# A two-layer attention and retention trunk: first rotation read from PSUM, a block's projections in column parts, and sines and weight squares issued at other steps

## The chip, the core and the metric

The kernel runs on one core of one Trainium2 chip. A core has five engines that each work through their own instructions in order and wait for each other by semaphores: PE (matrix products, with a separate row for its weight loads, PEld), DVE (vector work), ACT (scalar functions with lookup tables), POOL, and SP, which here only issues DMA transfers. The metric is device time in microseconds (us); lower is better.

## The reference

Two layers over 2048 tokens of width 1024, then a last norm. Each layer computes

```python
hn = rms_norm(x, norm_gain)
aq, ak, av, ag, rq, rk, rv, rg = split(hn @ w_in)      # eight sections of 512 columns
ya = chunked_rel_attention(aq, ak, av, rel_bias)       # 8 heads x 64, chunks of 64 tokens, own chunk + 8 before
yr = chunkwise_retention(rq, rk, rv, cos, sin)         # 4 heads x 128, rotary phases, decay, group norm
y = concat([ya * silu(ag), yr * silu(rg)])
x = x + y @ w_out
```

The retention turns rq and rk by angles that grow with the position: `[t1*c - t2*s, t1*s + t2*c]` on the two halves of a head's 128 columns. Everything is float32 in and out, so the kernel forms each float32 product from three half-precision products: high by high, low by high and high by low.

The weights are not used as they stand: the kernel scales each block of weights by the root of its mean square before it is cut into a high and a low half. So each weight section has to be squared and summed before it can be converted.

## The kernel before

**Tiling.** A layer l is worked in four column groups s, and a group holds one retention head and two attention heads. For each group the tokens are worked in four row blocks n of 512 tokens, each made of four token tiles of 128. A block (l, s, n) has two dense stages. `dense_T` (L608) makes four tiles with the columns on the partitions and 512 tokens along the row: j = 0 is q, 1 is k, 2 is rq, 3 is rk; each takes 24 matmuls (eight sections of the inner dimension, three half-precision products). `dense_V` (L738) makes four tiles, one for each token tile, that hold v, rv and the gates; 24 matmuls each (L752). The attention (`attention` L778: scores S at L800 and L801, output o at L820 to L822) and the retention (`retention` L884, its products r at L860) of the block before run between these matmuls. The first block (0, 0, 0) is special: `first` is set, and q and k are made in eight parts of 128 columns (L712), since the normalised and transposed token tiles hTh and hTl arrive one by one.

**Order.** All instructions are issued by one Python program, and each engine works in the order issued. A round is some eight matmuls. At the end of a round `tick()` (L598) calls the functions that `later(k, fn)` (L595) has put off by k rounds. Work for later blocks runs as generators that are pushed with a number of steps and pulled some steps a round: `prep_T`, `prep_V` and `prep_O` load, square, scale and split weights, `prep_Omax` (L494) does the squares of the output weights, `tables` (L83) makes the angles' cosines and sines for a row block and writes them to DRAM, and the norms of later token tiles. PE, DVE, ACT and POOL follow this order; the issues on SP follow it until the end of the first `dense_V` and are ordered by a planner afterwards.

**PSUM.** The dense tiles have two buffers (psD), the scores one (psS), small results four (psR); in the first block rq and rk also use psR. A dense_V tile is evacuated by ACT (L760 to L763) and then by three "rests" on DVE (L766, L768, L770), after which its buffer is free.

**The rotation.** For rq and rk (L656 to L703) ACT copies the tile out of PSUM to `raw` (L662). Two DMAs on SP swap its halves into `swp` (L666, L667). DVE multiplies raw by the cosine table tabc and swp by the sine table tabs and adds (three operations at L670), ACT makes the upper half-precision part (L673), DVE the lower (L676); rq gets a third part from ACT (L679), and rk is transposed by DMA into kt (L683). Tabc and tabs are read back from DRAM by two DMAs (L616, L617).

**Weight squares.** `sumsq` (L306) squares a section on ACT (L309) with a sum along the row; `lowp` (L314) casts the sum to bfloat16 on DVE (L316); `allsum` (L320) sums over partitions with a small matmul against ones (L323) and DVE reads the result (L325). The sections of the T weights (q, k, rq, rk) and of the V weights (v, rv, gates) are prepared this way. In `square` (T) the cast directly follows the square, and so it does in `prep_V`:

```python
self.sq[j] = lowp(sumsq(self.sts[j], nm, self.g.h[:, j]), nm)
```

For the output weights `prep_Omax` squares eight sections one after the other, and adds each sum to the one before on DVE (L504, L506).

## Time and profile before

| | us |
|---|---|
| median of 3 runs | 2094.44 (2092.88 to 2094.84) |
| the profiled execution | 2094.75 |
| its span | 2092.8, which leaves 1.95 outside it |
| PE busy | 2004.4 (96%) |
| DVE busy | 1343.8 (64%) |
| ACT busy | 1141.3 (55%) |
| POOL busy | 432.9 (21%) |

The chain of work that ended last is PE's for the most part, and the rest of it is waiting for DMA, DVE and ACT. How to read the rows in the prediction: in a timeline row stand the start, the duration, the engine, the line of the program, the operation, the result and what it is made from, its shape, and how many instructions the row holds; in brackets how long the engine had been idle before it and what released it. A row of the waits gives the total, the number and the longest. SPq is the queue on which SP issues DMAs. The matmul of 128x512 is followed by the next after 0.216 us although each lasts 0.38: they are pipelined.

### The profile page before, as it was taken

The numbers are of one execution on the slowest core, as the hardware profiler recorded it, in microseconds if no ns is written. First come the engines' busy times: TensorE is split into PE (matmuls) and PEld (weight loads), VectorE is DVE, ScalarE is ACT, GpSimd is POOL, SyncE is SP. The second block draws the span as 40 slices with busy tenths as digits, with TensorE's granted clock in tenths as the row PEclk, the third lists the DMA queues.
The fourth block names the chain that finished last, engine by engine and source line by source line (L and its number), as shares of the span: only waits on it lengthen the run. The fifth ranks groups of instructions, "written<-read, shape, count | busy, mean of one in ns | idle before, by whom it ended". The sixth has DMA issues, their size and how long they took to land.

```text
span 2092.8 us, 39599 instructions
## 1 busy us (share of the span) xinstructions
PE 2004.4 (96%) x14014; PEld 1049.4 (50%) x14014; DVE 1343.8 (64%) x4031; ACT 1141.3 (55%) x2522; POOL 432.9 (21%) x509
## 2 busy tenths in 40 slices
PE   6888999999999999998999999999999999998998
PEld 4344455555555555444444555555555555554443
DVE  7676666666656666576654666666666667656643
ACT  7455665556565654455444546554655565455432
POOL 1022222222122212121000222222222222222100
PEclk9999999999999999999999999999999999999999
DMA  8767674557476764599965556655655776558874
GB/s 247 171 127 162 136 166 114 115 112 159 110 169 133 161 166 99 113 211 260 219 185 113 120 102 142 130 121 106 155 123 118 178 156 162 117 100 183 212 199 123
DMA packets 645702, 313.65 MB, mean 150 GB/s; under 512 B 459232, under 2 KB 602080, under 8 KB 645504
## 3 DMA queue, kind: packets, MB, share of 16 engines
q1 hardware_dynamic: 645504, 311.12, 66.4%
q8 instruction: 110, 1.80, 0.4%
q14 instruction: 88, 0.72, 0.1%
HBM read 123.26 MB, written 41.98 MB: 79 GB/s over the span
## 4 chain that ended last, share of the span: by engine, by line
PE 55%; DMA 7%; DVE 5%; ACT 3%; issue 1%; SPq 1%; POOL 0%; POOLq 0%; DVEq 0%; ACTq 0%
PE dT L731 18%; PE dV L752 15%; PE dO L1105 12%; DMA pT<-pq 2%; PE r L860 2%; PE S L801 2%; PE S L800 2%; PE o L820 1%; PE o L821 1%; PE o L822 1%; DVE sc L804 1%; DMA swp<-rot 1%; DMA yhy<-rhy 1%; ACT sc L807 1%; ACT pq L809 1%
## 5 line engine op out<-in xcount | busy, mean ns | idle before, releaser
L810 POOL TENSOR_TENSOR pq<-sc,pq 128x640 f16<-128x640 f32 (+4 forms) x256 | 323.8, 1265 | 1175.9 <-issue 590.7
L807 ACT ACTIVATE sc<-sc,mq,cT 128x640 f32<-128x640 f32 (+4 forms) x256 | 218.5, 853 | 558.1 <-DVE mq L806 413.7
L752 PE MATMUL dV<-whV,hTh 128*128 128x512 f16 x1024 | 354.5, 382 | 13.0 <-DVE gt L770 12.8
L731 PE MATMUL dT<-hTh,whT 128*128 128x512 f16 x1008 | 349.4, 382 | 14.7 <-DMA hTh<-hTl 9.6
L752 PE MATMUL dV<-wlV,hTh 128*128 128x512 f16 x1024 | 354.1, 381 | 0.0
L752 PE MATMUL dV<-whV,hTl 128*128 128x512 f16 x1024 | 354.0, 381 | 0.0
L731 PE MATMUL dT<-hTl,whT 128*128 128x512 f16 x1008 | 346.6, 379 | 0.0
L731 PE MATMUL dT<-hTh,wlT 128*128 128x512 f16 x1008 | 346.6, 379 | 0.0
L752 PEld LDWEIGHTS <-hTh 128*128 128x128 f16 x2048 | 197.3, 98 | 227.7 <-DVE gt L770 16.4
L731 PEld LDWEIGHTS <-whT 128*128 128x128 f16 x2016 | 192.9, 98 | 221.6 <-issue 24.1
L804 DVE CUSTOM_DVE_ANT_0 sc<-S,bias 128x640 f32<-128x640 f32 (+4 forms) x256 | 188.4, 736 | 78.8 <-PE S L801 61.1
L1105 PE MATMUL dO<-whO,yly 128*128 128x512 f16 x512 | 194.1, 379 | 2.4 <-DMA yly<-rly 2.4
L1105 PE MATMUL dO<-whO,yhy 128*128 128x512 f16 x512 | 194.0, 379 | 1.2 <-DVE gt L770 0.6
L1105 PE MATMUL dO<-wlO,yhy 128*128 128x512 f16 x512 | 194.0, 379 | 0.0
L809 ACT ACTIVATE pq<-sc 128x640 f16<-128x640 f32 (+4 forms) x256 | 171.5, 670 | 10.9 <-DMA pT<-pq 3.0
L1105 PEld LDWEIGHTS <-yhy 128*128 128x128 f16 x1024 | 99.6, 98 | 115.1 <-issue 0.8
L752 PEld LDWEIGHTS <-hTl 128*128 128x128 f16 x1024 | 99.7, 98 | 105.0 <-issue 2.8
L800 PE MATMUL S<-k,q 128*128 128x128 f16 (+3 forms) x592 | 143.1, 268 | 7.9 <-DVE mq L804 7.9
L731 PEld LDWEIGHTS <-wlT 128*128 128x128 f16 x1008 | 97.2, 98 | 101.8 <-issue 1.1
L820 PE MATMUL o<-v,pT 128*128 128x65 f16 x1120 | 129.6, 193 | 10.2 <-DMA pT<-pq 9.7
L801 PE MATMUL S<-k,q 128*128 128x128 f16 (+3 forms) x592 | 130.5, 268 | 0.0
L820 PEld LDWEIGHTS <-pT 128*128 128x128 f16 x1120 | 105.3, 97 | 49.2 <-DMA pT<-pq 21.3
(350 smaller groups left out, 3352.7 us busy)
## 6 DMA issues: line engine op xcount, KB each, us to landing
q<-qq SPq DMA_DIRECT2D x128, 128.0 KB, 2.7
yyy<-y_d SPq DMA_DIRECT2D x32, 512.0 KB, 4.6
stT<-in_w_in_dram SPq DMA_DIRECT2D x27, 512.0 KB, 4.8
stV<-in_w_in_dram SPq DMA_DIRECT2D x26, 512.0 KB, 4.5
k<-kk SPq DMA_DIRECT2D x128, 64.0 KB, 2.0
swp<-rot SPq DMA_DIRECT2D x64, 128.0 KB, 2.5
tabc<-tab SPq DMA_DIRECT2D x32, 256.0 KB, 2.7
tabs<-tab SPq DMA_DIRECT2D x32, 256.0 KB, 2.9
```

The costliest lines, as they stand in the source:

```text
L731: pe.matmul(ps, w_[:, j, kt, :], h_[:, kt, :], start=(m == 0), stop=(m == 23))
L752: pe.matmul(ps, h_[:, kt, a * P:(a + 1) * P], w_[:, kt, :], start=(m == 0), stop=(m == 23))
L800: pe.matmul(o, st.q[:, hx, 0, cs], k_, start=True, stop=False)
L801: pe.matmul(o, st.q[:, hx, 1, cs], k_, start=False, stop=True)
L804: dve.tensor_tensor_reduce(out=v, in0=S[:, 0:w], in1=g.bias[hx][:, 640 - w:640], scale=1.0, scalar=-3.0e38, op0=ALU.add, op1=ALU.max, accu ...
L807: act.activation(v, v, AF.Exp, bias=m[:, 0:1], scale=g.c[:, 0:1])
L809: act.activation(pq[:, 0:w], v, AF.Copy)
L810: pool.tensor_tensor(pq[:, w:2 * w], v, pq[:, 0:w], op=ALU.subtract)
L820: pe.matmul(o[:, 0:65], u.p[:, b, :], v_[:, 0:65], start=(b == 0), stop=False)
L821: pe.matmul(o[:, 0:64], u.p[:, b, :], v_[:, 65:129], start=False, stop=False)
L860: pe.matmul(out_, w_, m_, start=(i == 0), stop=(i + 1 == len(pairs)))
L1105: pe.matmul(ps, h_[:, kt, :], w_[:, kt, :], start=(m == 0), stop=(m == 23))
```

## The change

1. In the first block the rotation reads rq and rk straight from PSUM (`first_rotation`). ACT's copy and the two swap DMAs for each are gone. DVE multiplies the PSUM tile by the cosine table, makes the two swapped halves with one product each of 64 partitions (`sine`), adds, and makes the lower part; ACT makes the upper and the third part as before.
2. The block (0, 0, 1) makes q and k in the eight column parts that the first block has, with 24 matmuls of 128x128 each; the attention's scores and the retention go between them at other places than before.
3. The first decayed scores (`decayed` for token tile 0) are issued from a `later(11, ...)` inside the first dense_V rather than after the first attention unit of the next block.
4. `tables` yields once more ahead of its sines for the row blocks after the first.
5. The cast of a weight section's square is issued a step after the square, for the T weights and for the next group's V weights. The matmul that uses it is issued where it was.
6. `prep_Omax` is pushed a stage earlier with more steps, loads two sections ahead, lets ACT write each sum to a column of its own, and sums the eight columns with one DVE reduction at the end.

```diff
@@ -118,6 +118,8 @@
         dve.tensor_tensor(k, k, ang, op=ALU.add)
         dve.tensor_scalar(k, k, HALF_PI, PI_CL, op0=ALU.add, op1=ALU.min)
         yield
+        if n:
+            yield
         act.activation(r, ang, AF.Sin)
         act.activation(k2, k, AF.Sin)
         yield
@@ -367,7 +369,10 @@
 
         def square(self, j):
             nm = f"{self.nm}{j}"
-            self.sq[j] = lowp(sumsq(self.sts[j], nm, self.g.h[:, j]), nm)
+            self.sq[j] = sumsq(self.sts[j], nm, self.g.h[:, j])
+
+        def cast(self, j):
+            self.sq[j] = lowp(self.sq[j], f"{self.nm}{j}")
 
         def scale(self, j):
             nm = f"{self.nm}{j}"
@@ -389,6 +394,7 @@
             yield
             w.square(j)
             yield
+            w.cast(j)
             yield
             yield
             w.scale(j)
@@ -439,8 +445,10 @@
         m1 = [None] * 2
         for j in range(2):
             yield
-            m1[j] = lowp(sq(j), f"{nm}{j}")
-            yield from rest(3)
+            m1[j] = sq(j)
+            yield
+            m1[j] = lowp(m1[j], f"{nm}{j}")
+            yield from rest(2)
             m = allsum(m1[j], f"{nm}{j}")
             sv, iv[j] = norm_scale(m, f"{nm}{j}", gains[l].i)
             yield from cv(j, sv)
@@ -450,9 +458,9 @@
         yield
         yield from rest(1)
         m3 = sq(3)
+        yield
         dve.tensor_tensor(m2, m2, m3, op=ALU.add)
         m2 = lowp(m2, f"{nm}2")
-        yield
         yield from rest(2)
         m = allsum(m2, f"{nm}2")
         sv, iv[2] = norm_scale(m, f"{nm}2", gains[l].i)
@@ -493,19 +501,28 @@
 
     def prep_Omax(l, go):
         nm = f"O{l}"
-        mm = b2.tile([P, 1], F32, tag="omax", name=f"omax{nm}")
-        st = load_sec(w_out[l, :, 0:P], f"{nm}m0")
+        ms = b2.tile([P, KT], F32, tag="omax", name=f"omax{nm}", bufs=1)
+        st = []
+
+        def load(j):
+            t_ = w4.tile([P, KT, P], F32, tag="w4", name=f"st{nm}m{j}")
+            sp.dma_start(t_, w_out[l, :, j * P:(j + 1) * P].rearrange("(k p) c -> p k c", p=P))
+            st.append(t_)
+
+        load(0)
+        load(1)
+        yield
         for j in range(KT):
-            yield
-            m1 = sumsq(st, f"{nm}m{j}", None)
-            if j + 1 < KT:
-                st = load_sec(w_out[l, :, (j + 1) * P:(j + 2) * P], f"{nm}m{j + 1}")
-            if j == 0:
-                dve.tensor_copy(mm, m1)
-            else:
-                dve.tensor_tensor(mm, mm, m1, op=ALU.add)
-        mm = lowp(mm, nm)
-        for _ in range(4):
+            if j + 2 < KT:
+                load(j + 2)
+            yield
+            act.activation(st[j], st[j], AF.Square, accum_out=ms[:, j:j + 1])
+            yield
+        yield
+        m1 = b2.tile([P, 1], F32, tag="m1", name=f"m1{nm}", bufs=4)
+        dve.tensor_reduce(m1, ms, axis=AX.X, op=ALU.add)
+        mm = lowp(m1, nm)
+        for _ in range(2):
             yield
         m = allsum(mm, nm)
         sv, iv = norm_scale(m, nm)
@@ -624,6 +641,42 @@
             else:
                 later(1, fn)
 
+        def first_rotation(j, ps, rot):
+            if j == 2:
+                st.rq = rot
+                later(1, tab_load)
+                own = rot[:, 1:3].rearrange("p a c -> p (a c)").bitcast(F32)
+            else:
+                st.rk = rot
+                own = b1.tile([P, 512], F32, tag="qq", name=f"raw{nm}")
+            st.swp = []
+
+            def cosine():
+                dve.scalar_tensor_tensor(out=own, in0=ps, scalar=2.0 ** -16, in1=st.tabc, op0=ALU.mult, op1=ALU.mult)
+
+            def sine(half):
+                if half == 0:
+                    st.swp = b1.tile([P, 512], F32, tag="swp", name=f"swp{nm}_{j}")
+                i_, o_ = slice((1 - half) * 64, (2 - half) * 64), slice(half * 64, half * 64 + 64)
+                dve.scalar_tensor_tensor(out=st.swp[o_], in0=ps[i_], scalar=-2.0 ** -16, in1=st.tabs[i_], op0=ALU.mult,
+                                         op1=ALU.mult)
+
+            def tokens():
+                st.kt = b1.tile([P, KT, P], F16, tag="ktok", name=f"kt{nm}")
+                sp.dma_start_transpose(out=st.kt, in_=rot.rearrange("p a c -> p (a c)"))
+
+            d = 2 * j
+            later(d, cosine)
+            later(d, lambda: sine(0))
+            later(d + 1, lambda: sine(1))
+            later(d + 2, lambda: dve.tensor_tensor(own, own, st.swp, op=ALU.add))
+            later(d + 3, lambda: act.activation(rot[:, 0], own, AF.Copy))
+            later(d + 4, lambda: dve.tensor_tensor(rot[:, 1], own, rot[:, 0], op=ALU.subtract))
+            if j == 2:
+                later(d + 5, lambda: act.activation(rot[:, 2], rot[:, 0], AF.Copy, scale=2.0 ** -11))
+            else:
+                later(d + 6, tokens)
+
         def evacuate(j, ps):
             if j == 0:
                 st.q = b2.tile([P, 2, 2, 512], F16, tag="q", name=f"q{nm}")
@@ -655,6 +708,9 @@
             else:
                 w = 5 - j
                 rot = b2.tile([P, w, 512], F16, tag=f"rot{j}", name=f"rot{nm}_{j}")
+                if first:
+                    first_rotation(j, ps, rot)
+                    return
                 if j == 2:
                     raw = rot[:, 1:3].rearrange("p a c -> p (a c)").bitcast(F32)
                 else:
@@ -682,7 +738,7 @@
                         st.kt = b1.tile([P, KT, P], F16, tag="ktok", name=f"kt{nm}")
                         sp.dma_start_transpose(out=st.kt, in_=rot.rearrange("p a c -> p (a c)"))
 
-                    d = 5 if j == 2 and first else 3
+                    d = 3
                     later(d, turned(raw, raw, st.tabc, ALU.mult))
                     later(d + 1, turned(swp, swp, st.tabs, ALU.mult))
                     later(d + 2, turned(raw, raw, swp, ALU.add))
@@ -691,16 +747,14 @@
                     if j == 2:
                         later(d + 5, third)
                     else:
-                        later(d + 5 if first else 11, tokens)
+                        later(11, tokens)
 
                 if j == 2:
                     st.rq = rot
                     swap()
-                    if first:
-                        later(1, tab_load)
                 else:
                     st.rk = rot
-                    later(8 if first else 2, swap)
+                    later(2, swap)
 
         if first:
             ps = [psD.tile([P, 512], F32, tag="dense", name=f"dT{nm}_{j}") for j in range(2)]
@@ -715,7 +769,23 @@
             for j in range(2):
                 evacuate(j, ps[j])
                 yield
-        for j in range(2 if first else 0, 4):
+        parts = (l, s, n) == (0, 0, 1)
+        if parts:
+            ps, m = [None] * 2, 0
+            for (j, a) in ((0, 0), (0, 1), (0, 2), (1, 0), (1, 1), (1, 2), (0, 3), (1, 3)):
+                if a == 0:
+                    ps[j] = psD.tile([P, 512], F32, tag="dense", name=f"dT{nm}_{j}")
+                cs = slice(a * P, (a + 1) * P)
+                for i in range(24):
+                    w_, h_ = ((g.h, hh), (g.l, hh), (g.h, hl))[i // KT]
+                    pe.matmul(ps[j][:, cs], w_[:, j, i % KT, :], h_[:, i % KT, cs], start=(i == 0), stop=(i == 23))
+                    m += 1
+                    if m % 32 == 0 and m < 192:
+                        yield
+                if a == 3:
+                    evacuate(j, ps[j])
+            yield
+        for j in range(2 if first or parts else 0, 4):
             if j == 2 and not first:
                 tab_load()
             if first:
@@ -849,8 +919,6 @@
             yield
             if hx == 1:
                 next(ret, None)
-            elif a == 0 and (l, s, n) == (0, 0, 0):
-                decayed(l, s, n, g, st, 0)
             pipe.append(lambda u=u: pv(u))
             yield
 
@@ -1401,6 +1469,8 @@
                         push(prep_T(l, s + 1, grp(l, s + 1)), 25)
                     else:
                         push(prep_O(l, 0, gO[0], go), 9)
+                if n == 2 and s == 2:
+                    push(prep_Omax(l, go), 22)
                 if n == NS - 1 and s == 1 and l + 1 < DEPTH:
                     gain_load(l + 1)
                 if not first:
@@ -1408,14 +1478,12 @@
                 if n == NS - 1 and s == NSW - 1:
                     us = []
                     push(wout_first(l, go, us), 10)
-                if n == 2 and s == 2:
-                    push(prep_Omax(l, go), 13)
                 if n == NS - 1:
                     if s + 1 < NSW:
                         push(prep_V(l, s + 1, grp(l, s + 1)), 23)
                     else:
                         push(prep_O(l, 1, gO[1], go), 9)
-                if (n, s) == (0, 0) and not first:
+                if (n, s) == (0, 0):
                     later(11, lambda n=n, g=g, st=st: decayed(l, s, n, g, st, 0))
                 run(dense_V(l, s, n, g, st), att, 24 if n == NS - 1 and s < NSW - 1 else 12)
                 if first:
```

More of the change, by code (lines that the diff above doesn't have):

```diff
@@ L134, in tables @@
         yield
-    TAB_STEPS = 19
+    TAB_STEPS = 20
     class St:
```

## The prediction

> **What bounds the kernel now.** I read the page first, then PE's waits over the whole run, then the table by stage, then the timelines of the stages in which PE waited.
>
> ```profile
> span 2092.8 us, 39599 instructions
> PE 2004.4 (96%) x14014; PEld 1049.4 (50%) x14014; DVE 1343.8 (64%) x4031; ACT 1141.3 (55%) x2522; POOL 432.9 (21%) x509
> PE dV L752 <- DVE gt L770: 12.8, 6, 4.9
> PE dT L731 <- DMA hTh<-hTl: 9.6, 1, 9.6
> PE msT L323 <- DVE mbT L316: 3.3, 3, 1.9
> 50.00:75.00 25.00, 19.27 (x90) 8.49 (x87) 16.29 (x31) 12.99 (x27) 1.90 (x5) 0.93 0.84 188
> ```
>
> PE is busy for 96% of the span, so 88 us can be won at most by any reordering. The waits say where: one single wait of 9.6 us for a transposed token tile (hTh), 12.8 us in six waits for the rests of an output tile, and waits of one or two us at the small matmuls that sum the weights' squares. The table (span, then busy time of PE, weight load, DVE, ACT and POOL, the granted clock, DMA share, GB/s) has the largest at 50 to 75 us, in the first row block: 19.27 of 25 busy, and a clock of 0.93. The change touches those stages and the squares, and nothing in the output projection. The other rows of the sum are shown part by part below; the sum is made against the profiled execution's 2094.75 us (span 2092.8 and 1.95 outside it), 0.3 above the median of the runs, 2094.44.
>
> **First stage: rotation from PSUM, and column parts.**
>
> ```profile
> 64.14 0.38 PE L752 MATMUL dV<-whV,hTl 128*128 128x512 f16 x1
> 68.89 0.38 PE L752 MATMUL dV<-wlV,hTh 128*128 128x512 f16 x1
> 78.91 3.26 PE L731 MATMUL dT<-hTh,whT 128*128 128x512 f16 x8 [9.64 <-DMA hTh<-hTl]
> 91.90 0.38 PE L731 MATMUL dT<-hTh,whT 128*128 128x512 f16 x1
> 34.33 0.61 PE L712 MATMUL dT<-hTh,whT 128*128 128x128 f16 x8
> 35.67 0.61 PE L712 MATMUL dT<-hTh,whT 128*128 128x128 f16 x8
> 62.17 0.68 DVE L670 TENSOR_TENSOR swp<-swp,tabs 128x512 f32<-128x512 f32 x1
> 62.77 0.28 DVE L766 SCALAR_TENSOR_TENSOR v<-dV,v 128x128 f16<-128x128 f32 x1
> 63.23 0.41 DVE L770 SCALAR_TENSOR_TENSOR gt<-gt,dV 128x256 f32<-128x256 f32 x1
> 64.16 1.22 DVE L276 TENSOR_TENSOR hTl<-hTl,hTl 128x1024 f16<-128x1024 f32 x1
> 78.11 0.69 DVE L670 TENSOR_TENSOR raw<-raw,tabc 128x512 f32<-128x512 f32 x1 [7.20 <-DMA swp<-raw]
> 72.41 0.59 SPq L667 DMA_DIRECT2D swp<-raw  x1
> 73.10 1.53 SPq L236 DMA_TRANSPOSE hTh<-hTl  x1
> ```
>
> PE finishes the first block's dV at 68.89 and then has nothing: the second block's q and k need all four token tiles, and the last one's transpose stands on SP behind the swaps of the first rotation. The change cuts q and k into eight parts of 128 columns; six of them need only the first three token tiles. It also takes the four swap DMAs off SP and forms the swapped halves on DVE.
>
> The parts cost PE little: 24 matmuls 128x128 take 35.67 − 34.33 = 1.34 us, against 24 × 0.216 / 4 = 1.29 for a quarter of the wide tile (rows 64.14 to 68.89: 22 steps, 0.216 each).
>
> The rotation costs DVE. It gains a cosine and two sines for each of rq and rk (six operations where L670 had four products), at a pitch of 0.60 (62.17 to 62.77). Worse, six rotation operations now stand ahead of the rests of the second dV tile, where two stood. Those rests (62.77 to 63.64) free the PSUM buffer of the fourth dV tile, which starts on PE right behind them, at 64.14. So it starts 4 × 0.60 = 2.4 later, and I add 0.3 for the angle table: 66.8. A forward step (the decayed scores of the first block, three small matmuls) now stands on PE after 16 matmuls of that tile, thus at 66.8 + 16 × 0.216 = 70.3, and waits for rk's lower half. On DVE there stand, from the rests' end at 66.4: a sine 0.6, the low half of a token tile 1.2 (row 64.16), two steps of rotation 1.2, the third tile's rests 0.9, five small table steps, estimated at 1.7 (0.28 to 0.41 each, rows 62.77 and 63.23), and the lower half itself 0.6, in sum 6.2: 72.6. PE thus loses 2.3 there, and ends dV at 72.6 + 0.2 + 8 × 0.216 = 74.5 instead of 69.1. The six parts run without a wait to 74.5 + 6 × 1.34 + 0.3 for two S = 82.9. The last token's transpose, without the swaps' two issues and with one x load behind it, is issued some 1.6 before 73.10, long enough before. The last two parts end at 85.8. The next tile then waits for the first one's evacuation, which stands on ACT behind the table's sines and an exp, and for its rest on DVE: 86.7 to 87.9, 87.25 as the middle. Against 91.90 that is a gain of 4.65. Ends: if DVE's reads from PSUM cost half as much again, ten operations × 0.3 take 3.0 of it, and 1.6 are left; if DVE's chain holds PE nowhere, 2.7 + 2.3 come on top, 9.6.
>
> Both new stalls lie between these two rows of a pause and what followed it:
>
> ```profile
> 140.13 1.89 PE L731 MATMUL dT<-hTh,whT 128*128 128x512 f16 x8 [2.21 <-issue]
> 204.90 3.40 PE L731 MATMUL dT<-hTh,whT 128*128 128x512 f16 x8 [2.81 <-DMA hTh<-rhn]
> ```
>
> After 2.21 us of idling eight matmuls took 1.89, after 2.81 they took 3.40, at half speed. I charge the stalls of 2.7 and 2.3 nothing; if both were followed by slow matmuls, that is 2 × 1.5 = 3.0, again a first stage of 1.6. The Trainium skill (TensorE: Matmul & The Clock Gate, HAM oscillation — how this bites in real kernels) puts the limit at pauses of over about 3.4 us; by that rule neither stall costs anything beyond itself and the 4.65 stands. The row at 204.90 speaks against so high a limit, so the 1.6 stays in the range.
>
> **Second stage: sines later.**
>
> ```profile
> 124.36 1.28 ACT L121 ACT_TABLE_LOAD   x1
> 126.28 0.26 ACT L760 ACTIVATE v<-dV 128x128 f16<-128x128 f32 x1
> 126.54 1.28 ACT L761 ACT_TABLE_LOAD   x1
> 129.54 0.61 PE L752 MATMUL dV<-whV,hTh 128*128 128x512 f16 x1 [4.88 <-DVE gt L770]
> 132.50 0.59 PE L752 MATMUL dV<-whV,hTl 128*128 128x512 f16 x1
> 133.09 0.45 SPq L616 DMA_DIRECT2D tabc<-tab  x1
> 134.88 1.25 SPq L812 DMA_TRANSPOSE pT<-pq  x1
> 136.18 1.57 SPq L236 DMA_TRANSPOSE hTh<-rhn  x1
> ```
>
> Now ACT loads the sine's table and runs two sines before the evacuation (1.92), and reloads in the middle of it (1.28). The change puts the evacuation first: about 3.1 of the 4.88 go, and the eight slow matmuls behind it (0.43 apart, 129.54 to 132.50) run at full speed, 1.7 more. So PE reaches the next q tile 4.8 earlier. But that tile waited already, from 137.9 to 140.13. The view names no releaser; I read it as the transposed token tile, issued at 136.18 (the earlier one took from 73.10 to 78.91 to be used). Its issue stands on SP behind the table's eight writes and its two reads. The reads move behind it (133.09 to 134.88, 1.8), the writes do not. It arrives 1.8 earlier, PE stands there for 2.2 + 4.8 − 1.8 = 5.2, and by the row at 129.54 eight slow matmuls follow, 1.5 as at 204.90 (3.40 against 1.89). The stage is worth 1.8 − 1.5 = 0.3; I take 0.5, since the first stage's lead also brings the norms forward. Ends: −1 (later sines push the writes and the transpose back) and +2 (no slow matmuls). In the third block the same move lets the exp's correction stand behind fewer instructions, but the evacuation keeps the sines ahead of it: −0.3 to 0, −0.3 taken.
>
> **Casts of the weights' squares later.**
>
> ```profile
> 252.21 0.16 DVE L316 CAST mbV<-m1V 128x1 bf16<-128x1 f32 x1 [2.85 <-ACT whV L309]
> 253.87 0.16 PE L323 MATMUL msV<-mbV,ones 128*128 128x1 bf16 x1 [1.57 <-DVE ya L832]
> 281.65 0.16 PE L323 MATMUL msV<-mbV,ones 128*128 128x1 bf16 x1 [1.31 <-DVE ya L832]
> 366.04 0.41 DVE L770 SCALAR_TENSOR_TENSOR gt<-gt,dV 128x256 f32<-128x256 f32 x1
> 366.11 0.17 PE L323 MATMUL msT<-mbT,ones 128*128 128x1 bf16 x1
> 571.21 0.17 PE L323 MATMUL msT<-mbT,ones 128*128 128x1 bf16 x1
> 572.14 0.41 DVE L770 SCALAR_TENSOR_TENSOR gt<-gt,dV 128x256 f32<-128x256 f32 x1
> ```
>
> For the V weights DVE stands 2.85 at the cast, waiting for ACT's square, with work behind it for which PE then waits 1.57 and 1.31. Casting later lets that work pass: I take 1.2 and 0.65, since part of each wait is PE's own order; ends 0 and 2.9.
>
> For the T weights the cast moves too, but its matmul stays where it is on PE. In the order of instructions the casts of the third and fourth section now stand behind the rests of a dV tile (L766, L768, L770). In the first of the five fourth sections the matmul ran at 366.11, and the rests end at 366.45; with 0.16 for the cast PE waits 0.50. In the second it ran at 571.21 and the rests end at 572.55: 1.50. Taking their mean, 1.0, for all five gives −5.0. In the third sections the rests end at about the time of the matmul; I put them at 0.1 each, −0.5. Sum −5.5; ends −10 (ten at the mean) and 0, if another engine had held PE there anyway.
>
> **Output squares summed at the end.**
>
> ```profile
> 624.60 0.33 PE L860 MATMUL r<-rot,rot 128*128 128x128 f16 x3 [1.09 <-DVE dT L868]
> 627.88 0.18 PE L323 MATMUL msO<-mbO,ones 128*128 128x1 bf16 x1 [0.73 <-DVE yr L925]
> 1637.60 0.33 PE L860 MATMUL r<-rot,rot 128*128 128x128 f16 x3 [1.27 <-DVE dT L868]
> 1640.70 0.18 PE L323 MATMUL msO<-mbO,ones 128*128 128x1 bf16 x1 [0.55 <-DVE yr L925]
> ```
>
> Eight adds on DVE each wait for a square on ACT, and that for a load; the steps that PE needs next stand behind them on DVE (dT L868, yr L925). The adds become one sum at the end, and the loads start a tile earlier, two ahead. All four PE waits go, with the step before each (0.16 to 0.3): 1.25 + 0.90 + 1.43 + 0.71, and 0.3 of smaller ones: 4.6. Ends 2 and 4.6.
>
> **Sum.** 4.65 + 0.5 − 0.3 + 1.85 − 5.5 + 4.6 = 5.8: 2094.75 − 5.8 = 2089.
>
> **Rivals.**
> *The first stage comes whole.* The two stalls on DVE do not appear (rests and rotation change places in time, since SP brings the table 1.2 earlier without the swaps): 9.6 instead of 4.65, 2084. For it speaks that DVE idled 7.20 before 78.11; against it that this idle time lies after the stalls.
> *It does not do what it says: the lead is given back.* The second stage's q tile still starts near 140.1 because the SP queue (writes, transposes) sets it, and what the first two stages win is waited off there. Then 0.65 remains of the rest (−0.3 + 1.85 − 5.5 + 4.6): 2094. For it speaks the row 136.18, which follows the queue and not PE; against it that the queue's work hangs on ACT and DVE, which the first stage brings forward.
> *Slower: the casts behind the rests.* The other parts sum to 11.3. If the ten casts of the third and fourth T sections hold PE for more than 1.13 each, the change loses; above 1.55 it is slower by over 0.2%. The longest such wait in the profile is 1.9 (row msT): 10 × 1.9 − 11.3 = 7.7, 2102.5. For it speaks 1.50 at 571.21; against it 0.50 at 366.11.
>
> **How the numbers follow.** My forecast 0.50, the first stage whole 0.18, given back 0.19, casts 0.13. A measurement of this kernel tells 0.2% (4.2 us) from no change, so faster means under 2090.3. The forecast's own range is 2085 to 2092: I give 0.39 of its 0.50 to faster, 0.11 to same. Faster 0.39 + 0.18 = 0.57, same 0.11 + 0.19 = 0.30, slower 0.13. The range 2081 to 2097 leaves out the slower case and 0.05 below it.
>
> **What would show it.** Right: no wait of 9.6 before the second block, about 2.5 twice in the fourth dV tile, the third tile of the second block at about 87; an evacuation before the sines and a wait of about 5 for the token tile near 138; waits of about 1 at the ms matmul of fourth T sections; none at 624 and 1637. Wrong: the third tile later than 90, no wait at those matmuls, or a q tile still at 140.

## The result and the profile after

The changed kernel takes 2099.8 us (median of 20 runs) against 2094.64 (20 runs) for the kernel before. The ratio is 1.0027, with a 95% interval of 1.0018 to 1.0036: it is about 5.7 us slower, where 5.8 us faster was forecast.

The page and the waits of PE of the changed kernel (columns as before: total, number, longest):

```profile
span 2097.6 us, 39868 instructions
PE 2008.9 (96%) x14158; PEld 1057.3 (50%) x14158; DVE 1347.3 (64%) x4019; ACT 1139.4 (54%) x2520; POOL 432.3 (21%) x509
PE dV L822 <- DVE gt L840: 13.4, 7, 4.2
PE o L890 <- DMA pT<-pq: 12.3, 13, 2.3
PE msT L325 <- DVE mbT L318: 10.0, 12, 1.9
PE dT L801 <- DMA hTh<-rhn: 8.7, 2, 4.9
PE msO L325 <- DVE mbO L318: 1.3, 1, 1.3
```

The single wait of 9.6 for hTh is gone. In its place stand longer ones for later token tiles (8.7 in two), twelve waits for the casts of the T weights (10.0, where there were three with 3.3) and more waiting for transposed probabilities (pT). Those waits were the second longest in the kernel before, too, and the prediction did not quote them; here are its row and, from its page, the transfers of instructions over the DMA engines:

```profile
PE o L820 <- DMA pT<-pq: 9.7, 11, 2.2
q8 instruction: 110, 1.80, 0.4%
```

PE's idle time is nearly the same in the two profiles (span less busy: 88.4 before, 88.7 changed). What grew is its busy time, from 2004.4 to 2008.9. Part of the busy time runs at a granted clock of 0.5, when the matmuls of 128x512 follow each other after 0.43 us instead of 0.216: 23.4 us in the trace of the kernel before, 31.5 in that of the changed one.

The stages that the prediction went through, in the changed kernel's timeline of PE:

```profile
66.37 0.39 PE L822 MATMUL dV<-whV,hTh 128*128 128x512 f16 x1 [2.93 <-DVE gt L840]
68.16 0.63 PE L822 MATMUL dV<-wlV,hTh 128*128 128x512 f16 x1
72.51 0.23 PE L928 MATMUL r<-rot,rot 128*128 128x128 f16 x1 [0.72 <-DVE rot L674]
74.31 0.61 PE L781 MATMUL dT<-hTh,whT 128*128 128x128 f16 x8
86.70 0.38 PE L801 MATMUL dT<-hTh,whT 128*128 128x512 f16 x1 [0.79 <-DVE qq L687]
122.27 0.39 PE L822 MATMUL dV<-whV,hTh 128*128 128x512 f16 x1 [1.44 <-DVE gt L840]
133.92 3.57 PE L801 MATMUL dT<-hTh,whT 128*128 128x512 f16 x8 [4.86 <-DMA hTh<-rhn]
201.44 3.57 PE L801 MATMUL dT<-hTh,whT 128*128 128x512 f16 x8 [3.87 <-DMA hTh<-rhn]
1371.18 0.18 PE L325 MATMUL msT<-mbT,ones 128*128 128x1 bf16 x1 [1.93 <-DVE mbT L318]
```

Since the order of the dense tiles on PE is the same in both kernels, the starts of the same tile can be subtracted. This table is worked out from the two traces (minus: the changed kernel is ahead); the last column is what the prediction would have had.

```
place                                        lead, us     forecast
third tile of block (0,0,1)                    -5.20        -4.65
second tile of block (0,0,2)                   -4.05        -5.15
second tile of block (0,0,3)                   -2.45        -4.85
fourth dV tile of (0,0,3), V casts             -3.90
fourth tile of (0,1,0)                         -1.71        -6.7
before the output squares, (0,2,2)             +0.14
fourth tile of (0,3,0)                         +1.49
end                                            +4.81        -5.8
```

A lead in one trace is uncertain by 1 to 2 us. Seven other kernels below leave the first stage as it was, and they start the third tile of block (0,0,1) between 1.5 us earlier and 1.1 later than the kernel before. One that is the changed kernel up to this place is 2.9 ahead there and not 5.2.

The first stage came as forecast. Its lead was lost in the next two blocks, at places near 277 and 695 us where no forecast step stands, and at the casts.

### The profile page after: what moved, and what is told of

Same layout as the page of the kernel before. It is cut to its first block, busy times and chain, and to the rows that moved or that the text cites. A ratio compares the mean times of both kernels' runs of the same rounds, so it can differ in the third digit from the quotient of the medians.

```text
span 2097.6 us, 39868 instructions
## 1 busy us (share of the span) xinstructions
PE 2008.9 (96%) x14158; PEld 1057.3 (50%) x14158; DVE 1347.3 (64%) x4019; ACT 1139.4 (54%) x2520; POOL 432.3 (21%) x509
## 3 DMA queue, kind: packets, MB, share of 16 engines
q8 instruction: 111, 1.82, 0.4%
## 4 chain that ended last, share of the span: by engine, by line
PE 70%; DVE 9%; DMA 9%; ACT 6%; issue 3%; SPq 2%; POOL 1%; DVEq 0%; POOLq 0%; ACTq 0%
PE dT L801 24%; PE dV L822 20%; PE dO L1173 14%; DMA pT<-pq 3%; PE r L928 3%; PE S L870 2%; PE S L871 2%; DMA swp<-rot 2%; DVE sc L874 1%; ACT sc L877 1%; PE o L890 1%; PE o L891 1%; PE o L892 1%; ACT pq L879 1%; DMA toep<-rel_d 1%
## 5 line engine op out<-in xcount | busy, mean ns | idle before, releaser
L801 PE MATMUL dT<-hTl,whT 128*128 128x512 f16 x992 | 342.3, 380 | 0.0
L801 PE MATMUL dT<-hTh,wlT 128*128 128x512 f16 x992 | 342.3, 380 | 0.0
L870 PE MATMUL S<-k,q 128*128 128x128 f16 (+3 forms) x592 | 143.5, 269 | 8.3 <-DVE mq L874 8.3
L890 PE MATMUL o<-v,pT 128*128 128x65 f16 x1120 | 130.2, 194 | 13.8 <-DMA pT<-pq 12.3
L936 DVE SCALAR_TENSOR_TENSOR sh<-sh,state 128x128 f16<-128x128 f16 x120 | 96.1, 801 | 54.0 <-ACT sh L932 53.8
```

The source lines that it names most:

```text
L801: pe.matmul(ps, w_[:, j, kt, :], h_[:, kt, :], start=(m == 0), stop=(m == 23))
L870: pe.matmul(o, st.q[:, hx, 0, cs], k_, start=True, stop=False)
L890: pe.matmul(o[:, 0:65], u.p[:, b, :], v_[:, 0:65], start=(b == 0), stop=False)
L936: dve.scalar_tensor_tensor(out=dst[:, 1], in0=dst[:, 0], scalar=-2.0 ** 11, in1=src, op0=ALU.mult, op1=ALU.add)
```

## The experiments

Each ratio is to the kernel before on the same chip. First each part was undone or done alone.

**T casts undone; T casts alone.** The first is the changed kernel with `square` and `cast` joined again; the second is the kernel before with

```diff
-            self.sq[j] = lowp(sumsq(self.sts[j], nm, self.g.h[:, j]), nm)
+            self.sq[j] = sumsq(self.sts[j], nm, self.g.h[:, j])
...
             w.square(j)
             yield
+            w.cast(j)
             yield
             yield
```

> The changed kernel with one part undone: the T weights' casts directly behind their squares again. Theory: in the changed kernel's trace PE's lead over the kernel before shrinks by 8.5 us in sum at the third and fourth sections' matmuls (L325, waiting for L318), more than the 5.5 forecast; with the casts back these waits go and the kernel is 2099.8 - 8.5 = 2091, 0.2% faster than before. Rival: the casts cost only the forecast 5.5, and the rest of the loss is waits of PE for transposed probabilities (12.3 us in the changed kernel against 9.7): then 2094, no difference from before, with those waits still there.

> The kernel before with only the T weights' casts a step later. Theory: 2094.6 + 8.5 = 2103, slower by 0.4%, with about ten waits of 0.4 to 2.1 us at the msT matmul. Rival: 2094.6 + 5.5 = 2100.

Alone the casts cost: 1.0019 (1.0011 to 1.0028), 4.0 us. PE's waits for them became 6.8 in 12, where 3.3 in 3 stood. Undoing them gave 1.0015 (1.0005 to 1.0026), only 2.5 us under the changed kernel: the twelve waits went (3.3 in 3), but those for transposed probabilities rose:

```profile
PE o L886 <- DMA pT<-pq: 17.4, 14, 2.8
PE msT L325 <- DVE mbT L318: 3.3, 3, 1.9
```

So the casts do what the prediction said, near its size (4.0 alone, 5.5 forecast), and something else takes away most of what undoing them should win.

**The first stage alone**, and the same with the first decayed scores two rounds later (`later(13, ...)` for `later(11, ...)`).

> The kernel before with only the first rotation from PSUM, the column parts and the earlier first decayed scores. Theory: rq of the second block starts about 5.2 us earlier, as in the changed kernel, but the second block waits again for the last transposed token tile of the third block and gives about half back: 2092. Rival one: the lead stays whole to the end: 2089.5. Rival two: it is given back whole at that wait: 2094.6.

> The first stage alone (first rotation from PSUM, column parts), with the first decayed scores two rounds later, after 32 matmuls of the second block's parts. Theory: the wait of PE for rk's lower half (2.2 at L911 in the first-stage run) goes, since the parts' matmuls run meanwhile, and rq of the second block starts about 2 earlier: 2092.3 against 2094.3 for the first stage alone in the run before. Rival: what follows waits for the score's decay or for the transposed token tile, and the lead is the same.

Alone it wins 0.9985 (0.9974 to 0.9996), 3.1 us, and its lead at the third tile of the second block is 4.9. The later scores did not help: 1.0001 (0.9993 to 1.0010). The wait at the lower half went, but the third tile came 1.3 later and not 2 earlier. That expectation was wrong; the 1.3 itself lies within what single traces differ by at this tile.

**The V casts alone.**

```diff
-            m1[j] = lowp(sq(j), f"{nm}{j}")
-            yield from rest(3)
+            m1[j] = sq(j)
+            yield
+            m1[j] = lowp(m1[j], f"{nm}{j}")
+            yield from rest(2)
```

> The kernel before with only the V weights' casts a step later. Theory: the waits at 253.9 and 281.7 go (2.4 us by the changed kernel's trace), but the planner of SP then puts both loads of the bias rows (L564) directly ahead of the bias load that waits for them, so SP stands and a transpose of probabilities behind it comes late: 2.2 lost. Sum 0.2 faster, same. Forecast: 1.85 faster.

0.9987 (0.9978 to 0.9996), 2.7 us faster: better than the theory of that moment. The planner did put the two loads one behind the other, and SP stood for the bias load, yet PE lost nothing there.

**The output squares alone**, and with the small matmul four steps behind the cast (`range(4)` for `range(2)`, 24 steps for 22).

> The kernel before with only the output weights' squares summed at the end. Forecast: 4.6 us faster, 2090. Theory after the result: layer 1 wins 2.2 and layer 0 only 0.6, since there the small matmul waits 1.3 for the cast behind the reduction (msO in the waits): 2.8 faster, 2091.8, with one wait msO <- mbO in layer 0.

> The kernel before with the output squares summed at the end, but the small matmul four steps behind the cast instead of two. Theory: of the 2.7 that this part lost alone, the two waits of 1.8 at msO come from the matmul being only two steps behind the cast; they go, and the kernel is 3.6 faster than with the part as it is: 0.9 faster than before. Rival: the loss is the squares on ACT, which now stand directly ahead of an evacuation or an exp in the stage before: still 2 to 3 slower than before.

Both are slower, where 2.8 and 0.9 faster were expected: 1.0013 (1.0002 to 1.0023) and 1.0011 (1.0002 to 1.0020). PE's waits in the two timelines around the first layer's small matmul, first as changed, then with four steps:

```profile
614.27 0.39 PE L761 MATMUL dV<-whV,hTh 128*128 128x512 f16 x1 [0.81 <-DVE gt L779]
622.28 0.16 PE L323 MATMUL msO<-mbO,ones 128*128 128x1 bf16 x1 [1.65 <-DVE mbO L316]
```

```profile
613.56 0.39 PE L761 MATMUL dV<-whV,hTh 128*128 128x512 f16 x1 [0.81 <-DVE gt L779]
620.13 0.39 PE L761 MATMUL dV<-whV,hTh 128*128 128x512 f16 x1 [0.21 <-DVE gt L779]
622.77 0.20 PE L829 MATMUL o<-v,pT 128*128 128x65 f16 x1 [0.74 <-DMA pT<-pq]
```

The waits of before at 624 and 627 are gone. But the matmul now stands so close behind the cast that it waits 1.65, and a square on ACT (1.04 at 610.39) stands ahead of an evacuation for which PE waits 0.81; both come again in the second layer. With four steps the 1.65 goes, and the loss does not: waits for transposed probabilities rise from 11.3 to 15.6.

**The sines undone; the sines alone** (the `if n: yield` ahead of them, and the count of steps).

> The changed kernel with one part undone: the sines of the later angle tables at their earlier step. Theory: the move loses 2.3 us in the second block (the first-stage run keeps its lead through it, from 4.9 to 6.1, while the changed kernel falls from 5.2 to 4.1) and 1.9 in the third block: 4.2 faster than the changed kernel, 2095.6 against its 2099.8, with PE's wait for the transposed token tile in the second block back from 4.9 to about 2.4. Rival, the forecast: the move is worth 0.2, and the kernel stays at 2099.8.

> The kernel before with only the sines a step later. Theory: the wait of the evacuation falls from 4.9 to 1.5, but the transposed token tile does not come earlier, so PE waits for it instead, long enough for eight slow matmuls: 0 to 2 us gained in the second block, 1 to 2 lost in the third; same to 2 us slower. Forecast: 0.2 faster.

1.0019 (1.0007 to 1.0030) undone, and 1.0018 (1.0009 to 1.0026) alone, 3.8 us slower. Alone, the stage itself went as said:

```profile
126.75 0.39 PE L754 MATMUL dV<-whV,hTh 128*128 128x512 f16 x1 [1.44 <-DVE gt L772]
138.33 3.35 PE L733 MATMUL dT<-hTh,whT 128*128 128x512 f16 x8 [4.79 <-DVE r L882]
```

3.4 of the evacuation's wait went, and 2.6 came back as a longer wait ahead of the next q tile (the view names DVE as its releaser here), followed by eight matmuls in 3.35. By the second tile of the block (0,0,3) this kernel is level with before (0.2 ahead). The rest of its 3.8 arose later, and these runs do not say where. Undone, the wait for token tiles fell from 8.7 to 4.9, but the waits for transposed probabilities came to 16.9. The ratio fell from 1.0027 to 1.0019, and those intervals overlap: not the 4.2 expected, and not to be told from no gain.

**The winning parts together**, also with the output squares at four steps.

> The two parts that won alone, together: first stage and later casts of the V weights' squares, all else as in the kernel before. Theory that the parts add: 3.1 + 2.7 = 5.8 faster than before. Rival: they share the same time (both are waited off at the first transpose of probabilities in the fourth column group, as the first stage's lead partly was): 3 faster.

> First stage, later casts of the V weights, and the output squares with the matmul four steps behind the cast. If the parts add: first_v less 0.9.

They did not add: 1.0008 (0.9997 to 1.0019) and 1.0006 (0.9995 to 1.0016). The two parts that won 3.1 and 2.7 alone win nothing together (the theory had 5.8, the rival 3), and their trace holds 17.7 us of waits for transposed probabilities.

**The number of transfers.** In every profile with the first stage so far PE lost time near 695, and in none without it. The first stage takes four transfers away, so four idle ones were put back:

```diff
+        if (l, s, n) == (0, 1, 1):
+            scr = dp.tile([4, 64, 512], F32, name="scr")
+            for i in range(4):
+                sp.dma_start(scr[i], x[0:64, 0:512])
```

> The first stage alone, with four further transfers of 64 x 512 numbers (DRAM to DRAM, used by nothing) issued at the start of the block (0, 1, 1), as many and as large as the swaps that it took away. In the five profiles with the first stage PE lost 1.5 to 4.5 at the first transposes of the fourth column group, near 695, in the five without it nothing. If the number of earlier transfers sets how such a transpose is spread over the DMA engines, the loss goes; if it is the time at which it is issued, it stays.

> The kernel before with the four idle transfers at the start of the block (0, 1, 1). If the number of earlier transfers decides how the transposes near 695 are spread over the DMA engines, moving it by four should harm the kernel before: a loss of 1.5 to 4.5 at that place that it does not have now. If instead only the lead of the first stage makes these waits, nothing happens there: same time as before.

> The changed kernel with the four idle transfers. If the count decides, the loss of 2.3 near 695 goes, and PE's waits for transposed probabilities fall below 12.3: 2099.8 less about 2 to 4, 2097. If not: 2099.8.

> First stage and later casts of the V weights, with the four idle transfers. The two parts together were 0.08% slower than before, though alone they won 3.1 and 2.7; PE's waits for transposed probabilities were 17.7 against 9.7. If the count of transfers is what kept them from adding, these waits fall to about 8 and the kernel is 5 faster than before, which beats both kernels. If not: the same as before.

In the first of these the loss near 695 went, 0.9996 (0.9986 to 1.0006); in the other two with the first stage it stayed (1.7 us each), 1.0030 (1.0019 to 1.0041) and 0.9999 (0.9989 to 1.0009). The kernel before did not get it, 1.0006 (0.9997 to 1.0015). So that theory fell.

**Transfers of instructions.** What the waiting kernels shared was in the DMA rows: PE's own instructions come over the same DMA engines. The page of before counts 110 such transfers with 1.80 MB on the queue q8, 16 KB each, for 28,028 PE instructions (14,014 matmuls with a weight load each): one for some 256. The eight column parts add 144 matmuls, 288 instructions; that is one transfer and 32 instructions, so each later transfer starts 32 instructions earlier in the work. From the traces of all twenty kernels, for each transpose of probabilities, the time of its flight, from the end of its issue on SP to its landing; the first row has those during whose flight a q8 transfer ran, the last 0.3 us left out:

```
a q8 transfer in its flight    827 transposes   mean 3.17   over 3 us: 61%
none                          4293 transposes   mean 2.05   over 3 us:  5%
```

A longer flight is likelier to meet a transfer, and some places in the program could have both. Neither explains the difference: if only the first 1.0 us of each flight is looked at, it stays (412 transposes that meet one, mean 3.13, against 2.15), and at all 63 places where the same transpose meets one in some of the kernels and not in others, it is later where it does (3.15 against 2.23 on average). The test moves nothing but the count of instructions, by matmuls of one number ahead of the first real matmul, where PE waits for 5 us anyway:

```diff
+    pad = psS.tile([P, D], F32, tag="S", name="pad")
+    for i in range(112):
+        pe.matmul(pad[0:1, 0:1], ones, ones, start=True, stop=True)
```

112 of them are 224 instructions, 512 with the column parts: two whole transfers. 16 of them, in the kernel before, are the 32 by which the change is off. The order on SP is the same with and without them. The traces show the shift: behind the parts, the q8 transfers start 42 PE instructions earlier in the work than in the kernel before (median; 36 with the 16 matmuls in the kernel before), and within 2 of it in the two kernels that are padded to 512.

> The kernel before with 16 matmuls of one number ahead of the first real matmul, where PE waits 5 us anyway; with their weight loads 32 PE instructions. In the traces the DMA engines carry one transfer of 16 KB of instructions for every 256 PE instructions. In the nine profiles with a wait near 695 this transfer starts 0 to 1.8 us behind the issue of a transpose of probabilities, and the transpose lands 3.2 to 4.3 us behind its issue instead of 1.9 to 2.6; in the kernel before it starts only after the landing. The first stage adds 288 PE instructions, 32 more than one such transfer holds. Theory: these 32 alone bring the transfer 32 instructions earlier and the wait of 1.6 to 3 near 695 appears, with nothing else of the change made; the rest of the run changes too, as other transfers of instructions move. Rival: the earlier time of the first stage makes the wait; then nothing appears.

> The changed kernel with 112 such matmuls, 224 PE instructions: with the 288 of the column parts 512, twice what one transfer of instructions holds, so that the transfers stand where they stand in the kernel before. Theory: the wait of 2.5 near 695 goes; by the median 2 to 3 faster than the changed kernel, ratio to before about 1.0015. The padding itself may cost up to 1 at the start. Rival: the wait stays.

> First stage and later casts of the V weights, padded in the same way to 512 PE instructions. Theory: the wait of 3.0 near 695 goes and the two parts keep more of what they win alone: 3 to 5 faster than before. Rival: as without the padding, 1 slower than before.

The kernel before became slower, 1.0012 (1.0002 to 1.0022). The changed kernel came to 0.9995 (0.9986 to 1.0004): by the ratios 6.7 us better than without the padding, where some 2.5 were expected. The two winning parts came to 0.9969 (0.9957 to 0.9981), 6.5 us faster than before and 8.2 better than without the padding; their median, 2088.07 us against 2096.14, beats both kernels. In the rows near 695, first of the changed kernel (the transpose's issue, the waiting matmul, and the DMA queues from 692.6 to 696.5, its flight), then of the padded one (flight 693.6 to 696.2):

```profile
689.14 3.41 SPq L882 DMA_TRANSPOSE pT<-pq  x1
696.55 0.20 PE L890 MATMUL o<-v,pT 128*128 128x65 f16 x1 [2.33 <-DMA pT<-pq]
q1 hardware_dynamic: 1193, 0.68, 74.2%
q8 instruction: 1, 0.02, 1.7%
```

```profile
690.49 3.15 SPq L885 DMA_TRANSPOSE pT<-pq  x1
696.22 0.20 PE L893 MATMUL o<-v,pT 128*128 128x65 f16 x1 [1.00 <-DMA pT<-pq]
q1 hardware_dynamic: 1257, 0.50, 114.1%
```

With the transfer out of its flight the transpose lands 2.5 after its issue instead of 4.0, and PE waits 1.0 instead of 2.3. Over the run, the winning parts without padding (span 2093.2) and with it:

```profile
PE o L875 <- DMA pT<-pq: 17.7, 16, 2.8
```

```profile
span 2082.5 us, 40110 instructions
PE o L878 <- DMA pT<-pq: 8.5, 11, 2.3
```

So 9.2 of the 10.7 us between these two profiles are waits for transposed probabilities. In the changed kernel it is otherwise. Its profiles without and with padding are 4.5 us apart, and of its waits those for transposed probabilities fall by only 1.3 (12.3 without), those for the T casts by 3.2 (10.0 without):

```profile
PE o L893 <- DMA pT<-pq: 11.0, 14, 1.7
PE msT L328 <- DVE mbT L321: 6.8, 13, 1.9
```

The 3.2 are the waits at 1371 and 1579, which fall from 1.9 and 1.6 to 0.2 each; no transpose of probabilities near them meets a q8 transfer that explains it. And PE works 21.7 us at a granted clock of 0.5, where it worked 31.5 without the padding. One of the three half-speed stretches that are gone followed a wait for such a transpose (at 277); the other two followed the stall at 66 and a late transpose of another kind at 978. The clock is not a matter of this one execution: its mean over the runs is 0.9909 in the changed kernel and 0.9925 in the padded one, 0.9913 and 0.9935 for the two winning parts, and 0.9905 and 0.9896 for the kernel before without and with 16 matmuls.

One expectation missed: in the padded kernel before the wait near 695 did not appear. The transfer started 1.5 behind the issue, but the transpose had landed 2.1 behind it. Its waits for transposed probabilities rose elsewhere, from 9.7 to 13.9. The place is thus not fixed; the collisions are.

## Why the prediction was wrong

**The step that failed most is one it did not have.** The sum counted the time of the parts' matmuls (1.34 against 1.29 for a quarter) and put at nothing that 288 more PE instructions shift every later transfer of instructions. With the shift taken out the ratio is 0.9995 instead of 1.0027. That is 0.32%, some 6.7 us, more than half of the miss of 11.5 between −5.8 and +5.7. It was taken for granted that the change does nothing after the steps that it touches. That the shift makes the transposes late that meet a transfer is shown; for the changed kernel it is open how the 6.7 divides into such waits, the waits for casts and half-speed matmuls. A padding by 256 instructions, which would leave the transfers where they are, was not run; that the padding helps by itself is unlikely, since 16 of its matmuls made the kernel before slower.

The Trainium skill (Runtime: NRT & Kernel Launch, Instruction fetch mechanics) says that instructions come in blocks of 16 KiB, 256 instructions, and that crossing a block is mostly hidden. The size agrees with the 110 transfers of 1.80 MB. It does not speak of data that is in flight at that time, and there the traces show a cost: the transposes that meet such a block take 3.17 instead of 2.05.

The terms of the sum, one by one, with the padded changed kernel's leads (worked out like the table above, so uncertain by 1 to 2 us each) as the size without that shift:

- **First stage, 4.65.** Right: 4.6 padded, 5.2 as changed; over the twelve traces with the first stage and the eight without it, the mean lead differs by 4.2. The stall ahead of the fourth dV tile was 2.93 (2.7 forecast). Slow matmuls did follow it (0.43 apart at 68.16), for which the sum charged nothing; the wait for the lower half was shorter for it (0.72, 2.3 forecast). In six other kernels the same stall lasted 2.7 to 3.5 and no slow matmuls followed, so that they did here was a matter of the execution. The rival "comes whole" is out. Over all twenty traces, a half-speed stretch began during the pause of PE or within 3.4 us behind it for 7 of 158 pauses of 1.4 to 2.0 us, 25 of 60 of 2.0 to 2.5, 34 of 43 of 2.5 to 3.4, and 69 of 79 longer ones. The Trainium skill (TensorE: Matmul & The Clock Gate, HAM oscillation — how this bites in real kernels) puts the limit at pauses of about 3.4 us; by these counts the limit is not sharp, and 3.4 is too high to be safe here.
- **Second stage, +0.5, and third block, −0.3.** Wrong by about 4, and mostly in the third block: the padded kernel goes from 4.62 ahead at the third tile of (0,0,1) to 0.64 ahead at the second tile of (0,0,3). 1.3 of this go ahead of the second stage, where PE waits 1.82 instead of 0.91 for a step of the attention on DVE, and no term has it. The stage itself, to the second tile of (0,0,2), loses 0.4; in the changed kernel it wins 0.2. Its mechanism was right (the evacuation's wait down to 1.44, the token tile's up to 4.86, slow matmuls behind). The third block loses 2.3, in the changed kernel 1.6: its wait grew from 2.81 to 3.87 where the prediction let it stand, and a half-speed stretch of 6.8 us follows it instead of one of 3.4. With the first stage and the sines where they were, no kernel loses more than 0.3 in that block, and with the sines moved the four that have both lose 1.6 to 2.3. The rival "given back" had the amount but not its place: the q tile did not stay near 140, it started at 133.92.
- **V casts, 1.85.** Right in direction, larger: 2.4 in the padded trace, 2.7 alone.
- **T casts, −5.5.** Near: 5.0 in the padded trace, 4.0 alone by the ratio. In the changed kernel the third sections at 1371 and 1579 waited too and cost 2.1 and 1.7, where 0.1 each had been put; padded and alone they do not. The slower rival, all ten at over 1.55, did not happen: the casts alone do not decide.
- **Output squares, 4.6.** Wrong. The four waits went, as said; new ones came, in each layer (0.81 at the evacuation, 1.65 at the matmul that is issued two steps behind the cast). Alone the part loses 2.7; in the padded kernel it wins 1.2. The step "all four PE waits go" looked at what the adds held, and not at what the squares on ACT and the shorter distance would hold next.

With the shift taken out the change is even with the kernel before: 0.9995, interval 0.9986 to 1.0004. So the prediction fell short twice: some 7.6 us of its sum were not there (4.2 around the second stage and the third block, 3.4 at the output squares), and what was there went to the shift. Not settled: where the sines alone lose 3.8 when their stage is level; why the third sections wait in the changed kernel and not in the padded one; and how much of each single part's ratio comes from transposes that meet a transfer at other places. Only three padded kernels were measured.

## What to carry to other kernels

Where a kernel is bound by PE and waits for short transfers, count the instructions that an edit adds to PE as well as their time: what is left over after whole instruction transfers (here 256 instructions) moves every later one. In the three pairs measured here that alone was worth 0.1 to 0.4%. Before a part is judged, try it padded so that the transfers stand where they stand in the kernel before; two parts that win alone and not together can be a sign of it. Look at PE's busy time as well as its waits: a pause can cost again as half-speed matmuls. And a step moved earlier or later is to be read from the instruction that stands behind it at its new place.

## What the runs showed of the hardware

PE's instruction stream uses the same DMA engines as the data: one transfer of 16 KB for about 256 instructions (110, 111 and 112 transfers for 28,028, 28,316 and 28,540 instructions). A transpose of probabilities that meets one lands 3.17 us after its issue on average, another 2.05. Sixteen matmuls of one number, in a time in which PE waits anyway, made the kernel before 0.12% slower (interval 0.02 to 0.22), and 112 made the changed one 0.32% faster by the ratios. Pauses of PE of 1.4 to 2.0 us came with a half-speed stretch in 7 of 158 cases, those of 2.0 to 2.5 in 25 of 60, those of 2.5 to 3.4 in 34 of 43; all the half-speed stretches between the start and the end of the program last 3.41 us or a multiple of it.
